# A diffusion layer on one core: the first convolution piece behind the query steps, the key weights loaded with the query projection

## The chip, the core and the metric

The kernel runs on one core of a Trainium2 chip. A core has a matrix engine (TensorE, PE in the rows; its weight loads are PEld), three engines for elementwise work (VectorE is DVE, ScalarE is ACT, GpSimd is POOL), SyncE (SP), whose queue here issues nearly all loads from memory, and 16 DMA engines that carry them. Each engine runs its own list of instructions strictly in the order in which it was written. The metric is the device time of one execution in microseconds (us): 1972.51 us before, the median of three runs (1969.02 to 1973.7).

## What is computed

One layer for 512 latent tokens of width 1024, with 256 context tokens as extra keys. Cut to what the change touches:

```
h  = modulate(rms_norm(x, norm1_g), sh1, sc1);  u = h @ w_in
q  = rms_norm(u[q part]) @ w_uq                # 16 heads of 64 + 32; the 32 are rotated (rope)
ckv = rms_norm(u[kv part]) of latent and context tokens;  kn, v = ckv @ w_ukv
attn = softmax(q k^T) v                        # per head, 768 keys
y  = a * sigmoid(g)                            # a, g: two projections of h, 1024 channels each
y  = depthwise convolution of y over the tokens, width 31, then layer norm, silu, @ w_pw
x  = x + g1 * ((gate_a * (attn @ w_o) + gate_c * y) @ w_out)
# then: norm, expert retrieval (PEER) and a final norm
```

## The kernel before

Tokens stand in four tiles of 128, in two groups of two tiles. Channels stand on the partitions in eight chunks of 128 (k). Group 0 goes through attention and the merge of its branches first, then its expert part is routed and its gathers run beside group 1; the last third of the time is a dense pass over all experts for group 1. Products that need high precision are split: a float32 tile is cast to a short form on ScalarE (line 107), the rest is taken on VectorE (line 108), and three matmuls (lines 128 to 130) stand for one.

Around the change the code goes through these steps.

- `query_in` (`qsteps[0]`): the query projection of group 0, its norm, and four transposes (line 287) into `cqT`.
- The key path: `kvn` is normed and transposed (lines 449 and 453), giving `ckvT`, and the rotated key parts in the four `KT` tiles.
- `query_half` (`qsteps[1:]`, two of them): for each half of the heads, two loads of `wuq` (line 296), eight matmuls of 384 columns (line 301; each shows as two records in the trace), copies of `qn` on ScalarE (302), six rotation instructions for each of two token tiles on VectorE (310 to 315), eight transposes for each tile (line 321), and copies to `QT` (324 on VectorE, 325 on ScalarE).
- `conv_in`: eight pieces, one for each channel chunk m. A piece loads and splits `w_cg` and `w_ca`, runs 96 matmuls of 256 columns (lines 128 to 130), a sigmoid (220), the product `glu` (221 on VectorE), the first tap on ScalarE (223), 29 taps on VectorE (line 225, `yo<-glu,cvw,yo`), and the last tap in two halves (227).
- `attention`: loads `wkn` and `wv`, then 32 units of one head and one token tile. For each pair of heads `keys` makes keys and values (478, 486); a unit has scores (497), a maximum on VectorE (499), an exponential on ScalarE (501), transposes (507) and the product with the values (522). A table of fillers says behind which unit other work is given: sixteen steps of the modulation matrix (`wm`, line 173; matmuls on line 176) at every second unit, convolution pieces at units 1, 5, 9 and so on, four gate chunks (565) at units 3, 9, 15 and 21.

The order in which the code gives its steps is not yet the order on the engines: a scheduler takes all instructions and writes each engine's list, earlier given steps first where they are ready. Buffers come from pools that are handed out in a ring, in the order of the code: in this part raw weights (`wt`, `wuq`, `wm`) share three buffers, so a load has to wait until the raw weight three before it has been used or split. SP's queue holds such a load, and everything behind it, until then. `big` takes from a ring of 14 buffers of 128x1024.

Of the kernel before, what the change touches and what calls it, by code (L numbers as in the profile page):

```python
# [45 lines left out]
PIECES, POFF = 1, 1  # L46
QPOS = (0, 0, 0)
GATES, GOFF, GSTEP = 4, 3, 6
LATE, N0, NU = 6, 0, 48

GROUPS = [[0, 1], [2, 3]]
# [20 lines left out]
def tile_layer(ctx, tc, a, out):  # L72
    nc = tc.nc
    te, ve, se, ge, sy = nc.tensor, nc.vector, nc.scalar, nc.gpsimd, nc.sync
# [18 lines left out]
    def big(name, dt=F32):  # L93
        return k4.tile([P, D], dt, name=name, tag="k4")
# [25 lines left out]
    def at(x, *i):  # L120
        return tuple(t[(slice(None),) + i] for t in x)
# [84 lines left out]
    def conv_in(y):  # L206
        def piece(m):
            glu = cvb_.tile([P, SEQ + 2 * HALF], F32, name="glu")
            ve.memset(glu[:, 0:HALF], 0.0)
            ve.memset(glu[:, SEQ + HALF:], 0.0)  # L210
            wg = wload(a["w_cg"], m)
            wa = wload(a["w_ca"], m)
            pg = ps1()
            pa = ps1()
            for o, w in ((pg, wg), (pa, wa)):
                for g, x in enumerate((hh, h2nd)):
                    for k in range(KC):
                        mm3(o[:, g * GT:(g + 1) * GT], at(w, k), at(x, k), k == 0, k == KC - 1)
            sg = sp.tile([P, SEQ], F32, name="sg", tag="c2", bufs=2)
            se.activation(sg, pg, AF.Sigmoid)  # L220
            ve.tensor_mul(glu[:, HALF:HALF + SEQ], pa, sg)
            yo = cvb_.tile([P, SEQ], F32, name="yo")
            se.activation(yo, glu[:, 0:SEQ], AF.Identity, bias=cvb[:, m:m + 1], scale=cvw[:, m, 0:1])  # L223
            for w in range(1, W - 1):
                ve.scalar_tensor_tensor(yo, glu[:, w:w + SEQ], cvw[:, m, w:w + 1], yo, op0=ALU.mult, op1=ALU.add)  # L225
            for o, c in ((y[:, m], slice(0, GT)), (yo[:, GT:], slice(GT, SEQ))):
                ve.scalar_tensor_tensor(o, glu[:, W - 1 + c.start:W - 1 + c.stop], cvw[:, m, W - 1:W], yo[:, c],
                                       op0=ALU.mult, op1=ALU.add)
            sy.dma_start(yd[:, m], yo[:, GT:])
        return [lambda m=m: piece(m) for m in range(KC)]  # L230

    def conv_norm(y):

        raw = [big("sT").rearrange("p (k t) -> p k t", k=4) for _ in range(2)]
        pm = ps2()
        for k in range(KC):
            te.matmul(pm[:, :GT], ones, y[:, k], start=k == 0, stop=k == KC - 1)
        mu = sp.tile([P, GT], F32, name="mu", tag="mu", bufs=2)
        se.mul(mu, pm[:, :GT], 1.0 / D)
        for q in range(2):  # L240
            yv = y[:, 4 * q:4 * q + 4]
            ve.tensor_sub(yv, yv, mu[:, None, :].to_broadcast([P, 4, GT]))
            se.activation(raw[q], yv, AF.Square)
        pv = ps2()
        for k in range(KC):
            te.matmul(pv[:, :GT], ones, raw[k // 4][:, k % 4], start=k == 0, stop=k == KC - 1)
        rd = sp.tile([P, GT], F32, name="rd", tag="mu", bufs=2)
        se.activation(rd, pv[:, :GT], AF.Sqrt, bias=eps_t, scale=1.0 / D)
        ve.reciprocal(rd, rd)
        hi, lo = [], []  # L250
        for q in range(2):
            yv = y[:, 4 * q:4 * q + 4]
            ve.tensor_mul(yv, yv, rd[:, None, :].to_broadcast([P, 4, GT]))
            for j in range(4):
                k = 4 * q + j
                se.activation(yv[:, j] if turn["split"] else raw[q][:, j], yv[:, j], AF.Silu, bias=lnb[:, k:k + 1], scale=lng[:, k:k + 1])
            if turn["split"]:
                h, l = two(yv, lambda: big("sp", F32R).rearrange("p (k t) -> p k t", k=4))
                hi.append(h)
                lo.append(l)  # L260
        return (hi, lo) if turn["split"] else (raw,)


    def queries(tiles, hx):

        cqT = sp.tile([P, 2, GT], F32, name="cqT", tag="sgm", bufs=2)
        QT = [[None, None] for _ in tiles]
        return QT, [lambda: query_in(tiles, hx, cqT)] + [lambda hf=hf: query_half(tiles, cqT, QT, hf) for hf in range(2)]
# [23 lines left out]
    def query_half(tiles, cqT, QT, hf):  # L292
# [10 lines left out]
        for i, t in enumerate(tiles):  # L303
# [21 lines left out]
            se.copy(qv[:, :, 1], pv[:, :, 1])  # L325
            QT[i][hf] = qt


    lc = ctx.enter_context(tc.tile_pool(name="lc", bufs=1))
    cvw = lc.tile([P, KC, W], F32)  # L330
# [10 lines left out]
    pieces = conv_in(y)  # L341
# [7 lines left out]
    with tc.tile_pool(name="tmp0", bufs=1) as t0:  # L349
# [55 lines left out]
        def split_h(g, o):  # L405
            for q in range(2):
                ks = slice(4 * q, 4 * q + 4)
                se.copy(o[0][:, ks], hT[g][q])
                ve.tensor_sub(o[1][:, ks], hT[g][q], o[0][:, ks])
# [13 lines left out]
            key_in(i)  # L423
        QT, qsteps = queries(GROUPS[0], hh)
        qsteps[0]()
        split_h(1, h2nd)
        sy.dma_start(cvw, a["cvw"])
        sy.dma_start(iota, a["iota"])
# [25 lines left out]
        for i in range(2):  # L454
            ve.tensor_copy(KT[i][1][:NOPE], pk2[:NOPE, :NKV])
            se.copy(KT[i][0][NOPE:HD], pk2[NOPE:HD, :NKV])
        for f in pieces[:1]:
            f()

    ep2 = early.enter_context(tc.tile_pool(name="ep2", bufs=1, side="right"))  # L460


    def attention(tiles, QT, fillers, wide=False):
        split = turn["split"]
        wk, wv = ((big if split else wtile)(n) for n in ("wkn", "wv"))
        sy.dma_start(wk, a["wkn"])
        sy.dma_start(wv, a["wv"])
        ah = [big("ah", F32R if split else F32).rearrange("p (k t) -> p k t", k=4) for _ in range(2)]
        if split:
            al = [big("al", F32R).rearrange("p (k t) -> p k t", k=4) for _ in range(2)]  # L470
# [87 lines left out]
    def gate(c, hv, sg):  # L558

        pg = ps1()  # L560
        for j, n in enumerate(("w_ga", "w_gc")):
            w = wload(a[n], c)
            for k in range(KC):
                mm3(pg[:, j * GT:(j + 1) * GT], at(w, k), hv[k], k == 0, k == KC - 1)
        se.activation(sg, pg, AF.Sigmoid)
# [410 lines left out]
    mf = mod_fillers()  # L976
    for f in qsteps[1:]:
        f()
    for f in pieces[1:PIECES]:
        f()  # L980
    fill = {}
    for q, f in enumerate(mf):
# [5 lines left out]
    def gate_ahead(g, c):  # L988
        rd = ready[g]
        if c % 2 == 0:  # L990
            rd["t"] = ep.tile([P, D], F32, name="sg", tag="hl", bufs=2) if g else big("sg")
        rd[c] = rd["t"][:, c % 2 * 2 * GT:(c % 2 + 1) * 2 * GT]
        gate(c, [at((hb,) if g else hh, k) for k in range(KC)], rd[c])

    for c in range(GATES):
        fill.setdefault(int(GOFF + c * GSTEP), []).append(lambda c=c: gate_ahead(0, c))
    aT = attention(GROUPS[0], QT, fill)
    conv.close()
    gp = ctx.enter_context(tc.tile_pool(name="gp", bufs=GPB))
    x1 = merge(GROUPS[0], hh, aT, lambda: conv_norm(y), ready=ready[0])  # L1000
# [4 lines left out]
    QT, qsteps = queries(GROUPS[1], (hb,))  # L1005
# [6 lines left out]
    peer["it"] = gathers(res)  # L1012
    later = route(res, h2T, 1, qat)
    sT = conv_norm(y)
    aT = attention(GROUPS[1], QT, {int(GOFF + c * GSTEP): [lambda c=c: gate_ahead(1, c)] for c in range(GATES)}, True)
    x1 = merge(GROUPS[1], (hb,), aT, lambda: sT, later, ready[1])
    later[-1]()
    full, h2T, parted = back(GROUPS[1], x1, False)
# [93 lines left out]
```

## Time and profile before

| what | value |
|---|---|
| median of 3 runs | 1972.51 us |
| the profiled execution | 1971.98 us |
| its span, first to last instruction | 1970.2 us |
| PE busy | 1785.6 us (91%) |
| weight loads (PEld) busy | 1426.8 us (72%) |
| VectorE busy | 1555.2 us (79%) |
| ScalarE busy | 774.2 us (39%) |
| GpSimd busy | 760.8 us (39%) |
| mean granted clock of TensorE | 0.96 of full |

The profile is one execution. A row of the timeline gives the start and the length of a run of like instructions on one engine, with the idle time ahead of it in brackets and what ended it. The ends of matmuls are modelled: neighbouring ones overlap in the rows, so the pace of TensorE is read from start to start. The granted clock is either full (2.4 GHz, shown as 1.00) or half (1.2 GHz, shown as 0.50); values between are means over a stretch that has both. In the rows tiles have their names without numbers.

### The profile page before, as it was taken

How to read it: one execution, taken by the hardware profiler on the slowest of the kernel's cores; microseconds unless marked ns; L12 is line 12 of the kernel's file. 1: busy time of each engine (PE TensorE's matmuls, PEld its weight loads, DVE VectorE, ACT ScalarE, POOL GpSimd, SP SyncE). 2: the span in 40 equal slices, each digit the busy share in tenths (PEclk: the TensorE clock that was granted, in tenths of full speed). 3: DMA queues.
4: the chain of work that ended last, by engine and by line, in shares of the span. 5: the costliest groups of instructions: out<-in, count | busy, mean ns of one | idle time of the engine just before them, and what ended most of it. 6: DMA issues, size and time to landing. Idle time of an engine off the chain costs nothing.

```text
span 1970.2 us, 29888 instructions
## 1 busy us (share of the span) xinstructions
PE 1785.6 (91%) x10952; PEld 1426.8 (72%) x10952; DVE 1555.2 (79%) x3122; ACT 774.2 (39%) x1147; POOL 760.8 (39%) x582
## 2 busy tenths in 40 slices
PE   6889999799987999699997889999999999999997
PEld 3667777597765766573652568788888788888886
DVE  3748989755698889897687874498996478999997
ACT  5345564543225553002111344333444444444444
POOL 0000000000045776554236882276562255655660
PEclk9889999999998999799999999999999999999999
DMA  8332333368486999899877659899999899999993
GB/s 315 106 112 89 121 118 103 120 202 274 140 321 240 347 334 347 304 388 351 274 263 263 250 216 307 295 387 400 386 396 339 307 350 385 399 398 386 395 399 157
DMA packets 179011, 555.67 MB, mean 282 GB/s; under 512 B 18984, under 2 KB 49192, under 8 KB 178608
## 3 DMA queue, kind: packets, MB, share of 16 engines
q1 hardware_dynamic: 105136, 285.29, 40.2%
q0 software_dynamic: 73728, 268.47, 36.9%
q8 instruction: 86, 1.41, 0.3%
q14 instruction: 61, 0.50, 0.1%
HBM read 533.23 MB, written 20.46 MB: 281 GB/s over the span
## 4 chain that ended last, share of the span: by engine, by line
PE 49%; DVE 17%; DMA 15%; issue 10%; POOL 6%; ACT 3%; SPq 0%; DVEq 0%; POOLq 0%; ACTq 0%
PE ps L129 9%; PE ps L128 9%; PE ps L130 9%; PE ps L126 6%; DMA g<-in_u_dram,ei 5%; DMA u<-in_ut_dram 4%; DVE scu L732 3%; PE ps L497 3%; POOL ohC L848 3%; PE acc L778 3%; POOL g L729 2%; DMA g<-in_v_dram,iT 2%; DVE wp L108 2%; PE ps L522 2%; PE acc L176 2%
## 5 line engine op out<-in xcount | busy, mean ns | idle before, releaser
L729 POOL DMA_INDIRECT g<-in_u_dram,ei x256 | 343.3, 1341 | 759.8 <-DVE tk L662 537.5
L732 DVE SCALAR_TENSOR_TENSOR scu<-g,h 128x1024 bf16<-128x1024 f32 x256 | 312.5, 1221 | 40.7 <-DMA g<-in_u_dram,ei 38.0
L128 PE MATMUL ps<-h2hi,wp 128*128 128x256 f32 x1024 | 290.9, 284 | 0.0
L130 PE MATMUL ps<-h2hi,wp 128*128 128x256 f32 x1024 | 289.7, 283 | 0.4 <-DVE wp L108 0.4
L129 PE MATMUL ps<-h2lo,wp 128*128 128x256 f32 x1024 | 289.6, 283 | 0.0
L789 POOL DMA_INDIRECT g<-in_v_dram,ei x128 | 207.0, 1617 | 143.7 <-DVE vsum L795 115.7
L107 ACT CAST wp<-u 128x1024 fp32r<-128x1024 f32 x128 | 134.2, 1049 | 278.8 <-DMA u<-in_ut_dram 168.2
L773 POOL DMA_INDIRECT g<-in_v_dram,iT x128 | 133.2, 1041 | 252.9 <-PE acc L778 213.6
L108 DVE TENSOR_TENSOR wp<-u,wp 128x1024 fp32r<-128x1024 f32 x128 | 156.4, 1223 | 86.1 <-ACT wp L107 85.1
L129 PE MATMUL ps<-v,wp 128*128 128x512 f32 x512 | 205.0, 400 | 8.9 <-DVE v L108 8.9
L128 PE MATMUL ps<-v,wp 128*128 128x512 f32 x512 | 203.6, 398 | 9.5 <-ACT v L107 6.8
L128 PEld LDWEIGHTS ps<-h2hi,wp 128*128 128x128 f32 x1024 | 195.8, 191 | 12.8 <-issue 10.9
L130 PE MATMUL ps<-v,wp 128*128 128x512 f32 x512 | 203.4, 397 | 0.5
L129 PEld LDWEIGHTS ps<-h2lo,wp 128*128 128x128 f32 x1024 | 196.1, 191 | 1.8
L130 PEld LDWEIGHTS ps<-h2hi,wp 128*128 128x128 f32 x1024 | 196.0, 191 | 0.6 <-DVE wp L108 0.6
L225 DVE SCALAR_TENSOR_TENSOR yo<-glu,cvw,yo 128x512 f32<-128x512 f32 x232 | 173.2, 749 | 4.6 <-ACT yo L223 0.9
L108 DVE TENSOR_TENSOR v<-v 128x1024 fp32r<-128x1024 f32 x128 | 156.5, 1223 | 24.0 <-ACT v L107 24.0
L795 DVE SCALAR_TENSOR_TENSOR vsum<-g,act,vsum 128x1024 f32<-128x1024 f32 x127 | 163.2, 1285 | 0.8
L107 ACT CAST v<-v 128x1024 fp32r<-128x1024 f32 x128 | 132.3, 1044 | 45.2 <-PE ps L129 39.0
L778 PE MATMUL acc<-g,Wz 128*32 128x512 f32 x512 | 104.2, 623 | 23.5 <-DMA g<-in_v_dram,iT 18.6
L129 PEld LDWEIGHTS ps<-v,wp 128*128 128x128 f32 x512 | 98.1, 192 | 33.4 <-DVE v L108 14.4
L128 PEld LDWEIGHTS ps<-v,wp 128*128 128x128 f32 x512 | 98.2, 192 | 29.2 <-ACT v L107 7.4
(306 smaller groups left out, 3650.8 us busy)
## 6 DMA issues: line engine op xcount, KB each, us to landing
v<-in_v_dram SPq DMA_DIRECT2D x128, 512.0 KB, 8.5
u<-in_ut_dram SPq DMA_DIRECT2D x128, 512.0 KB, 7.8
wm<-in_wmod_dram SPq DMA_DIRECT2D x48, 512.0 KB, 4.5
wt<-in_w_pq_dram SPq DMA_DIRECT2D x32, 512.0 KB, 4.2
Gd<-gb SPq DMA_DIRECT2D x16, 928.0 KB, 4.6
gr<-Gd SPq DMA_DIRECT2D x14, 1024.0 KB, 12.2
wt<-in_w_ga_dram SPq DMA_DIRECT2D x16, 512.0 KB, 4.4
wt<-in_w_gc_dram SPq DMA_DIRECT2D x16, 512.0 KB, 3.6
```

The source lines that it names most:

```text
L107: se.copy(h, raw)
L108: ve.tensor_sub(l, raw, h)
L128: te.matmul(o, w[0], x[0], start=start, stop=False)
L129: te.matmul(o, w[0], x[1], start=False, stop=False)
L130: te.matmul(o, w[1], x[0], start=False, stop=stop)
L225: ve.scalar_tensor_tensor(yo, glu[:, w:w + SEQ], cvw[:, m, w:w + 1], yo, op0=ALU.mult, op1=ALU.add)
L729: ge.indirect_dma_start(out=g, out_offset=None, in_=a["u"], in_offset=bass.IndirectOffsetOnAxis(ap=r["ei"][:, s:s + 1], axis=0))
L732: ve.scalar_tensor_tensor(scr, g, 1.0, r["h2"], op0=ALU.mult, op1=ALU.mult, accum_out=r["act"][:, s:s + 1])
L773: ge.indirect_dma_start(out=g, out_offset=None, in_=a["v"], in_offset=bass.IndirectOffsetOnAxis(ap=r["iT"][:, tk:tk + 1], axis=0))
L778: te.matmul(acc[32 * j:32 * j + 32, 512 * c:512 * c + 512], z[:, j, 31 - i:63 - i], gs[j][:, 512 * c:512 * c + 512], start=i == 0, stop=i ...
L789: ge.indirect_dma_start(out=g, out_offset=None, in_=a["v"], in_offset=bass.IndirectOffsetOnAxis(ap=r["ei"][:, s:s + 1], axis=0))
L795: ve.scalar_tensor_tensor(r["sum"], g, w, r["sum"], op0=ALU.mult, op1=ALU.add)
```

## The change

The line of the key weights' loads is taken out of `attention` into a function of its own, which is called right behind the query projection for group 0 and in front of `attention` for group 1, as before. The first convolution piece is no longer given inside the early block but behind the two query halves. Nothing is computed otherwise.

```
+    def key_weights(alloc):
+        ws = [alloc(n) for n in ("wkn", "wv")]
+        for w, n in zip(ws, ("wkn", "wv")):
+            sy.dma_start(w, a[n])
+        return ws
...
         qsteps[0]()
+        ws = key_weights(big)
         split_h(1, h2nd)
...
-        for f in pieces[:1]:
-            f()
...
-    def attention(tiles, QT, fillers, wide=False):
+    def attention(tiles, QT, fillers, ws, wide=False):
         split = turn["split"]
-        wk, wv = ((big if split else wtile)(n) for n in ("wkn", "wv"))
-        sy.dma_start(wk, a["wkn"])
-        sy.dma_start(wv, a["wv"])
+        wk, wv = ws
...
     for f in qsteps[1:]:
         f()
-    for f in pieces[1:PIECES]:
+    for f in pieces[:PIECES]:
         f()
...
-    aT = attention(GROUPS[0], QT, fill)
+    aT = attention(GROUPS[0], QT, fill, ws)
...
+                   key_weights(wtile), True)
```

PIECES is 1, so exactly one piece stands behind the query halves and the seven others stay in the table of fillers.

SP's queue from the load of the query projection to the third convolution piece's first load, before:

```order
L117 DMA wt<-in_w_q_dram 128x1024 x2
L427 DMA cvw<-in_cvw_dram 128x248
...
L117 DMA wt<-in_w_cg_dram 128x1024
L117 DMA wt<-in_w_ca_dram 128x1024
L296 DMA wuq<-in_wuq_dram 128x768 x4
L173 DMA wm<-in_wmod_dram 128x1024 x2
...
L466 DMA wkn<-in_wkn_dram 128x1024
L467 DMA wv<-in_wv_dram 128x1024
L117 DMA wt<-in_w_ca_dram 128x1024
```

The same stretch of SP's queue now (lines behind 326 have moved by a few numbers):

```order
L117 DMA wt<-in_w_q_dram 128x1024 x2
L331 DMA wkn<-in_wkn_dram 128x1024
L331 DMA wv<-in_wv_dram 128x1024
L434 DMA cvw<-in_cvw_dram 128x248
...
L296 DMA wuq<-in_wuq_dram 128x768 x4
L117 DMA wt<-in_w_cg_dram 128x1024
L117 DMA wt<-in_w_ca_dram 128x1024
L173 DMA wm<-in_wmod_dram 128x1024 x2
```

`wkn` and `wv` moved ahead of some twenty transfers, and the first piece's two weights moved from in front of the four `wuq` to behind them.

TensorE from the end of the query projection (line 287) to the first scores, before; ps_573 and ps_574 are the first convolution piece:

```order
L287 MATMUL ps_508<-ident,cqn 128x128 x2
L128 MATMUL ps_573<-hb,wp 128x256
...
L130 MATMUL ps_574<-h2nd_120,wp 128x256
L301 MATMUL ps_716<-wuq,cqT 128x384 x2
...
L176 MATMUL acc<-wm,ccz 32x512
L321 MATMUL ps_742<-ident,qn 96x128
...
L176 MATMUL acc<-wm,ccz 32x512 x2
L478 MATMUL ps_840<-ckvT,wkn 128x384
```

The same stretch of TensorE now; ps_701 and ps_702 are the first convolution piece:

```order
L287 MATMUL ps_508<-ident,cqn 128x128 x2
L301 MATMUL ps_570<-wuq,cqT 128x384 x2
...
L321 MATMUL ps_596<-ident,qn 96x128
...
L301 MATMUL ps_644<-wuq,cqT 128x384 x2
L128 MATMUL ps_701<-hb,wp 128x256
...
L130 MATMUL ps_702<-h2nd_120,wp 128x256
L481 MATMUL ps_840<-ckvT,wkn 128x384
L176 MATMUL acc<-wm,ccz 32x512
```

The query matmuls now come first and the 96 matmuls of the piece last before the keys; twelve matmuls on `wm` that stood among the query steps now stand behind the first keys.

VectorE in the query steps and the first attention units, before:

```order
L221 TENSOR_TENSOR glu<-ps_574,sg 128x512
L225 SCALAR_TENSOR_TENSOR yo<-glu,cvw,yo 128x512 x4
L310 TENSOR_TENSOR rt<-qn,rope 128x128
L225 SCALAR_TENSOR_TENSOR yo<-glu,cvw,yo 128x512
L311 TENSOR_TENSOR rt<-qn,rope 128x128
...
L324 COPY QT<-ps_821 96x4x128
L499 TENSOR_REDUCE st<-ps_861 128x1
L499 TENSOR_REDUCE st<-ps_876 128x1
```

VectorE in the query steps and the first attention units now:

```order
L310 TENSOR_TENSOR rt<-qn,rope 128x128
L311 TENSOR_TENSOR rt<-qn,rope 128x128
...
L324 COPY QT<-ps_675 96x4x128
...
L221 TENSOR_TENSOR glu<-ps_702,sg 128x512
...
L225 SCALAR_TENSOR_TENSOR yo<-glu,cvw,yo 128x512 x5
L502 TENSOR_REDUCE st<-ps_861 128x1
...
L502 TENSOR_REDUCE st<-ps_1042 128x1
L225 SCALAR_TENSOR_TENSOR yo<-glu,cvw,yo 128x512 x20
```

The 29 taps of the first piece no longer alternate with the rotations of the queries; they stand among the maxima of the first units, and one run of 20 (of the first and the second piece together) stands behind the third maximum. From the middle of the first group's attention on (the convolution's sixth piece) the lists of all engines are the same as before, and so are all lists behind it.

## Rows read from the trace of the kernel before

**Rows 1.** The chain of waits that ended last, 75 to 125 us: shares, then start, us, what

```profile
by line: DVE yo L225 26.2%; DMA wm<-in_wmod_dram 16.7%; DMA wkn<-in_wkn_dram 14.4%; PE ps L497 6.3%; PE acc L176 6.0%; PE ps L478 5.9%; DVE wp L108 4.6%; PE ps L486 4.2%; issue 2.9%; ACT yo L223 1.6%; DVE glu L221 1.4%; DVE QT L324 1.3%; DV
...
108.97 7.20 DMA wkn<-in_wkn_dram
```

**Rows 2.** By stretch, 75-116 us: length; busy PE, PEld, DVE, ACT, POOL; clock; DMA; GB/s

```profile
75.00:82.00 7.00, 7.00 (x24) 4.19 (x23) 5.73 (x11) 2.61 (x5) 0.00 (x0) 1.00 0.29 71
82.00:91.00 9.00, 4.63 (x20) 1.47 (x18) 9.00 (x21) 1.13 (x2) 0.00 (x0) 0.99 0.64 216
91.00:98.00 7.00, 6.73 (x16) 4.02 (x16) 6.81 (x11) 3.38 (x6) 0.00 (x0) 0.52 0.43 118
98.00:105.40 7.40, 3.36 (x18) 1.14 (x18) 7.40 (x17) 2.01 (x3) 0.00 (x0) 0.94 0.66 250
105.40:116.20 10.80, 5.75 (x16) 1.88 (x16) 2.99 (x9) 0.59 (x1) 0.00 (x0) 0.50 0.66 223
```

**Rows 3.** TensorE's timeline, 32 to 119 us: start, us, line, operation, count, idle before

```profile
32.16 3.64 PE L176 MATMUL acc<-wm,ccz 128*32 128x512 f32 x32
...
60.09 1.07 PE L287 MATMUL ps<-ident,cqn 128*128 128x128 f32 x4 [2.77 <-DVE cqn L284]
...
69.47 0.28 PE L128 MATMUL ps<-hb,wp 128*128 128x256 f32 x1
...
75.02 7.90 PE L301 MATMUL ps<-wuq,cqT 128*128 128x384 f32 x24
...
84.94 1.08 PE L321 MATMUL ps<-ident,qn 128*96 128x128 f32 x8
...
90.98 1.94 PE L321 MATMUL ps<-ident,qn 128*96 128x128 f32 x8 [3.32 <-DVE qn L315]
93.19 5.07 PE L301 MATMUL ps<-wuq,cqT 128*128 128x384 f32 x8 [0.27 <-ACT qn L302]
...
116.21 2.93 PE L478 MATMUL ps<-ckvT,wkn 128*128 128x384 f32 x4 [2.35 <-DMA wkn<-in_wkn_dram]
```

**Rows 4.** VectorE's timeline, taps in a row and taps between rotations

```profile
76.86 3.12 DVE L225 SCALAR_TENSOR_TENSOR yo<-glu,cvw,yo 128x512 f32<-128x512 f32 x4 [0.88 <-ACT yo L223]
...
80.09 0.75 DVE L225 SCALAR_TENSOR_TENSOR yo<-glu,cvw,yo 128x512 f32<-128x512 f32 x1
80.76 0.28 DVE L311 TENSOR_TENSOR rt<-qn,rope 128x128 f32<-128x128 f32 x1
```

**Rows 5.** Groups of instructions, 60 to 120 us: count, busy us, mean ns, idle before

```profile
L225 DVE SCALAR_TENSOR_TENSOR yo<-glu,cvw,yo 128x512 f32<-128x512 f32 x29 | 21.7, 747 | 1.0 <-ACT yo L223 0.9
```

**Rows 6.** SyncE's timeline: the query weights' and the key weights' issues

```profile
51.66 26.46 SPq L296 DMA_DIRECT2D wuq<-in_wuq_dram  x4
...
108.97 0.48 SPq L466 DMA_DIRECT2D wkn<-in_wkn_dram  x1
```

**Rows 7.** DMA issues, 30 to 130 us: count, size, median us to landing

```profile
wt<-in_w_cg_dram SPq DMA_DIRECT2D x3, 512.0 KB, 4.6
```

**Rows 8.** ScalarE's timeline: the first cast of the query projection's weight

```profile
45.98 1.05 ACT L107 CAST wp<-wt 128x1024 fp32r<-128x1024 f32 x1
```

**Rows 9.** Busy time by stretch, attention of the first group

```profile
123.10:138.40 15.30, 15.30 (x122) 14.01 (x121) 5.16 (x7) 9.01 (x13) 0.00 (x0) 1.00 0.12 36
138.40:170.80 32.40, 32.40 (x259) 27.27 (x256) 30.40 (x48) 20.16 (x31) 0.00 (x0) 1.00 0.32 95
170.80:180.00 9.20, 7.28 (x47) 4.03 (x45) 6.51 (x8) 5.09 (x8) 0.00 (x0) 0.81 0.53 195
180.00:271.00 91.00, 91.00 (x708) 74.36 (x709) 83.58 (x131) 49.54 (x79) 0.00 (x0) 1.00 0.30 95
271.00:346.00 75.00, 75.00 (x563) 56.80 (x562) 66.80 (x100) 40.00 (x64) 0.00 (x0) 1.00 0.35 113
```

**Rows 10.** VectorE's timeline: a maximum behind the second piece's last tap

```profile
170.80 0.96 DVE L499 TENSOR_REDUCE st<-ps 128x1 f32<-128x768 f32 x1 [0.60 <-PE ps L497]
```

**Rows 11.** SyncE's waits, 30 to 200 us: in total, times, longest

```profile
SPq L173 <- DVE wp L108: 57.9, 6, 20.5
```

More of the change, by code (lines that the diff above doesn't have):

```diff
@@ L1014, in tile_layer @@
     sT = conv_norm(y)
-    aT = attention(GROUPS[1], QT, {int(GOFF + c * GSTEP): [lambda c=c: gate_ahead(1, c)] for c in range(GATES)}, True)
+    aT = attention(GROUPS[1], QT, {int(GOFF + c * GSTEP): [lambda c=c: gate_ahead(1, c)] for c in range(GATES)},
+                   key_weights(wtile), True)
     x1 = merge(GROUPS[1], (hb,), aT, lambda: sT, later, ready[1])
```

## The prediction, made before the changed kernel ran

> **What bounds the kernel now.** I read the chain of waits first, for the stretch that the change rewrites, then the busy time by stretch, then the timelines of TensorE, VectorE and SyncE there. From 75 to 125 us the chain runs for 26.2% through the taps of the first convolution piece on VectorE, for 16.7% through loads of `wm` and for 14.4% through the load of `wkn` [rows 1]. So the reader is to see that TensorE isn't the bound there. Its busy time falls to 4.63 of 9.00 us, 3.36 of 7.40 and 5.75 of 10.80, and its clock to 0.52 and 0.50 in two of the stretches, while VectorE is busy for all of 82 to 105.4 us [rows 2]. The cause is the order on VectorE: each rotation of the queries stands between two taps, and TensorE waits 3.32 us for one of them; then the first keys wait 2.35 us for `wkn`, which SyncE issued only at 108.97 us [rows 3, 6]. The keys start at 116.21 us.
>
> From 123.1 us on it is otherwise: TensorE is busy all the time at full clock up to 170.8 us, and from 180 to 346 us again [rows 9]. VectorE is little used at first (5.16 of 15.3 us) and then nearly full: 30.40 of 32.4, 83.58 of 91, 66.80 of 75. Attention is thus bound by TensorE with VectorE close behind it.
>
> **The change part by part.**
>
> *The head, up to the first keys.* The four transposes behind the query projection start at 60.09 us, and TensorE's next matmul, now the first on `wuq`, can start at about 61.5. Before the keys it then has the following work, by pace from start to start. 32 records of line 301: 24 took 7.90 us at full clock, so 0.329 each and 10.5 in all. 32 records of transposes of the queries: 8 took 1.08, so 4.3. Twelve transposes of the key path at the same pace: 1.6. The 96 matmuls of the first piece: 48 ran from 69.47 to 75.02, so 0.116 each and 11.1 [rows 3]. That is 27.5 us. I add 1.3 us, since the clock is still at half after the idle 2.77 us (four records on `wuq` at the 0.634 each of the half-clock row less 0.329), and 1.5 us for the turns between ScalarE's copies and the rotations that nothing covers now. The keys then start at 61.5 + 30.3 = 91.8 us, 24.4 us earlier. Bounds: 27.5 without any stall (89.0), and 42 us with the whole query part at half clock (below).
>
> *The weights of the piece.* Its two loads now stand behind the four of `wuq`, and each waits for the raw weight three before it. The last `wuq` load waits for the first query matmuls (that row spans 26.46 us before, up to 78 us, for the same reason [rows 6]), so at about 66 us; `w_cg` follows when the second `wuq` is used, about 69, lands 4.6 us later [rows 7], and is split by 76. The piece begins on TensorE at about 79. The cover is 3 us; if it is gone, each further microsecond is one of the head.
>
> *The key weights.* They are issued right behind the query projection's weights, some 60 us before they are needed, into buffers of the ring that no one has used. They cost the query projection nothing as long as its weights still land in time: their first cast starts at 45.98 us without a wait [rows 8], some 12 us after the issue. The wait of 2.35 us goes. What is late next for the first keys is TensorE itself.
>
> *The moved taps.* 29 taps with 21.7 us [rows 5] leave the head and come among the first units. In a row, each feeding the next, they follow each other by 0.76 us (four from 76.86 to 79.89); ahead of a rotation the next instruction starts after 0.67 [rows 4]. So they cost 19.4 to 22.3 us of VectorE there, and I take the 21.7 of the row. The Trainium skill, "VectorE: DVE Perf Modes", section "The DRAIN you can't avoid", says that every instruction's pipeline has to run empty before the next starts, however they are chained; by it the order is worth nothing and the taps cost 21.7 us anywhere. The trace doesn't quite agree: 0.67 against 0.76. That moves the sum by 2.3 us at most.
>
> *How VectorE takes them.* The piece's matmuls end at 91.8; the product `glu` (0.7), the first tap on ScalarE (0.8) and a copy of keys ahead of it there put the first moved tap at 93.9. In front of the maximum that stands at 170.80 us before [rows 10], VectorE has the work that it had from 123.1 to 170.8 (5.16 + 30.40 = 35.6 us [rows 9]) and the 21.7: 57.3, so this maximum comes at 151.2 if VectorE never waits. TensorE alone would bring it sooner: keys at 91.8, first scores and maxima 5.4 us later at full clock (6.9 before, less half of the 2.93 of the keys' row, which ran at half clock), the same 47.7 us, and twelve matmuls on `wm` that stood in the head before and now come here, 24 records at 3.64 / 32 us [rows 3] or 2.7 us; together 147.6. VectorE decides by 3.6 us there. The gain at this point is 170.8 - 151.2 = 19.6 us.
>
> *From there to the end.* Up to the sixth piece the lists are nearly the same, and then they are the same. Before, 170.8 to 180 had a stop and half clock (7.28 of 9.20 busy, clock 0.81 [rows 9]), some 4 us of which may or may not come again; I take 1 as gained. From 180 us on TensorE was full with VectorE 8% and 11% behind, so VectorE has room for what it carries, and everything behind moves up by the same amount. Sum: 19.6 + 1, or 21 us.
>
> The profiled execution took 1971.98 us (span 1970.2), 0.5 below the median of the runs shown; 1972.0 - 21 = 1951.
>
> **The rivals.**
>
> *The query part runs at half clock (1963).* Before, these matmuls came right behind the 96 of the piece, which ran at full clock; now they come right behind an idle stretch. The records of line 301 took 0.634 us each in the row at 93.19 against 0.329, and the eight transposes at 90.98 took 1.94 against 1.08 [rows 3]. For: the clock fell to 0.50 to 0.52 in two stretches in which TensorE waited [rows 2]. Against: the query matmuls now wait on short ScalarE copies only, and 24 of them kept the full clock before. Price: 32 x 0.305 less the 1.3 already counted, and 32 x 0.11: 12 us, a gain of 9.
>
> *VectorE is the bound and takes the taps one for one (1969).* The gain of the head, 24.4, less 21.7 leaves 3 us. For: VectorE is at 92% from 180 to 271. Against: from 123.1 to 138.4 it had 10 us idle [rows 9], into which taps fit. The Trainium skill, "Perfetto Trace Analysis", section "Identifying the Most-Contended Engine", points the same way: matmul busy time says little of how near TensorE is to its limit, weight loads say more, and for VectorE the occupancy counts; here the weight loads have 74.36 of 91 us and VectorE 83.58, so by that rule VectorE is the bound of attention. By starts, though, the matmuls of the trace follow each other without gaps, so I give it little.
>
> *TensorE sets everything (1945).* 24.4 + 1.5 for the first scores at full clock - 2.7 for the twelve matmuls + 4 for the stop that does not come again: 27 us. It needs VectorE's interleaving to go better than the count of work says.
>
> *The splits of the weights come late, and it is slower (1981).* A split is an instruction on VectorE in line with the taps; now a run of 20 taps, 13 to 15 us, stands ahead of some, and each late split holds its raw buffer and with it SyncE's whole queue. SyncE waited 57.9 us in six waits for such splits already before, 20.5 in the longest [rows 11], mostly hidden. If the next three pieces each stop TensorE for the mean of 9.7 us, 29 us are lost and 20 gained: 9 slower. It decides from the point at which a piece's second weight isn't split when its first 48 matmuls end. Against: the code's order gives the early splits ahead of the run of 20.
>
> *The change doesn't act (1969 to 1972).* The queries would stay late because their own `wuq` loads come late. The last of these loads waits for the first query matmuls, not for the piece, so little speaks for it; it shares a chance with the one-for-one case, which gives the same time.
>
> **How the numbers follow.** The forecast 0.60, half clock 0.16, VectorE one for one or no effect 0.09, TensorE alone 0.10, late splits 0.05. The forecast's own range is a gain of 15 to 26 us, 1946 to 1957. To hold eight in ten the range takes in the half-clock case and TensorE alone: 1943 to 1966; left out are the one-for-one case, the slow one and the tails, some 17%. Faster by over 0.3% (5.9 us, about what a measurement can tell from no change) are the forecast, TensorE alone, nearly all of the half-clock case and a part of the one-for-one case: 0.87. Within 0.3% is the rest of that case, 0.08; slower, the late splits, 0.05.
>
> **What would show it.** In the profile after, the first keys start at 90 to 93 us and wait for no load; the query matmuls stand at 61 to 79 us with a clock near 1.00 after the first 3 us; VectorE is busy without a break from about 94 to 151 us; the maximum behind the second piece's last tap stands near 151; from the sixth piece on every row stands about 21 us earlier. It is wrong if the keys start behind 100 us, if TensorE has waits of several microseconds for splits or exponentials between 100 and 180 us, or if what is gained at the keys has shrunk below 10 us by 180 us of the run before.

## The result, and the profile after

The changed kernel takes 1952.89 us, the median of four runs (1949.24 to 1957.35), beside 1973.11 for four runs of the kernel before on the same chip: ratio 0.9895, 95% interval 0.987 to 0.9921. The forecast was 1951, range 1943 to 1966. A second measurement of the same kernel gave 1955.15 beside 1976.19, ratio 0.9897 [0.9869, 0.9926]. By medians the gain is 20.2 and 21.0 us; 21 was predicted.

The profiled execution was the longest of its four, 1957.35 us (span 1955.5), and that of before lay 1.1 us under the median of the four. Single executions of one kernel differ by several microseconds, so below I compare places in the program.

TensorE's timeline after (start, length, line, operation, count, idle before), from the transposes behind the query projection to the first keys; it answers to [rows 3]:

```profile
60.16 0.70 PE L287 MATMUL ps<-ident,cqn 128*128 128x128 f32 x4 [2.04 <-DVE cqn L284]
61.30 2.16 PE L301 MATMUL ps<-wuq,cqT 128*128 128x384 f32 x4 [0.44 <-DVE cqT L289]
...
65.69 4.73 PE L301 MATMUL ps<-wuq,cqT 128*128 128x384 f32 x14
70.56 1.05 PE L321 MATMUL ps<-ident,qn 128*96 128x128 f32 x8
...
72.97 4.04 PE L301 MATMUL ps<-wuq,cqT 128*128 128x384 f32 x12
76.54 0.57 PE L128 MATMUL ps<-hb,wp 128*128 128x256 f32 x1
...
90.31 0.81 PE L481 MATMUL ps<-ckvT,wkn 128*128 128x384 f32 x2
```

The query matmuls follow right behind the transposes, the piece's first matmul comes at 76.54, and the keys start at 90.31 without a load in front of them, 25.9 us earlier than at 116.21. From 61.30 on no row of the stretch, shown or not, has an idle time in brackets.

SyncE's timeline after, which answers to [rows 6, 7]:

```profile
33.65 1.53 SPq L331 DMA_DIRECT2D wkn<-in_wkn_dram  x1
...
41.23 26.27 SPq L296 DMA_DIRECT2D wuq<-in_wuq_dram  x4
69.80 0.33 SPq L117 DMA_DIRECT2D wt<-in_w_cg_dram  x1
74.45 0.33 SPq L117 DMA_DIRECT2D wt<-in_w_ca_dram  x1
```

The key weights are now under way at 33.65 us. The piece's weight is issued at 69.80; the last `wuq` still waits for the first query matmuls.

Busy time by stretch after (length; PE, PEld, DVE, ACT, POOL; clock; DMA; GB/s). These answer to [rows 2, 9]:

```profile
60.00:75.00 15.00, 14.26 (x59) 9.50 (x60) 10.21 (x31) 6.08 (x11) 0.00 (x0) 0.89 0.23 61
75.00:82.00 7.00, 6.88 (x49) 5.80 (x48) 5.71 (x16) 3.48 (x6) 0.00 (x0) 1.00 0.75 234
82.00:92.00 10.00, 10.00 (x76) 8.64 (x75) 1.92 (x2) 3.95 (x5) 0.00 (x0) 1.00 0.30 100
92.00:104.00 12.00, 12.00 (x83) 9.53 (x82) 11.73 (x16) 9.77 (x16) 0.00 (x0) 1.00 0.38 132
104.00:124.00 20.00, 20.00 (x163) 16.09 (x161) 19.79 (x29) 8.99 (x13) 0.00 (x0) 1.00 0.34 107
124.00:138.00 14.00, 11.22 (x79) 6.60 (x72) 13.33 (x24) 8.21 (x16) 0.00 (x0) 1.00 0.51 163
138.00:152.00 14.00, 14.00 (x113) 12.84 (x113) 12.19 (x21) 5.54 (x8) 0.00 (x0) 1.00 0.14 46
...
160.00:251.00 91.00, 90.45 (x708) 74.16 (x706) 84.00 (x131) 48.90 (x76) 0.00 (x0) 1.00 0.37 124
```

From 92 to 138 us VectorE is all but full (44.85 of 46 us). TensorE is full too, but for 2.78 us between 124 and 138, which it spends in four waits for ScalarE: 1.05 and 0.56 for copies of keys, 0.79 and 0.39 for exponentials. Then TensorE leads again. VectorE's timeline after shows what stood in front in that gap, and the maximum that answers to [rows 10]:

```profile
93.20 3.90 DVE L225 SCALAR_TENSOR_TENSOR yo<-glu,cvw,yo 128x512 f32<-128x512 f32 x5
...
112.07 0.95 DVE L502 TENSOR_REDUCE st<-ps 128x1 f32<-128x768 f32 x1
112.94 13.33 DVE L225 SCALAR_TENSOR_TENSOR yo<-glu,cvw,yo 128x512 f32<-128x512 f32 x20
...
128.50 0.95 DVE L502 TENSOR_REDUCE st<-ps 128x1 f32<-128x768 f32 x1
...
138.35 0.95 DVE L502 TENSOR_REDUCE st<-ps 128x1 f32<-128x768 f32 x1
...
140.99 6.27 DVE L225 SCALAR_TENSOR_TENSOR yo<-glu,cvw,yo 128x512 f32<-128x512 f32 x8
...
150.49 0.96 DVE L502 TENSOR_REDUCE st<-ps 128x1 f32<-128x768 f32 x1 [0.53 <-PE ps L500]
```

Twenty taps stand in one row, the last taps of the first piece in turn with taps of the second, and the fourth maximum is behind them. Against the same maximum of before, the first ten come earlier by 26.1, 25.9, 27.0, 13.9, 22.9, 20.1, 20.3, 24.7, 23.2 and 23.0 us. So the row of taps takes 13 us from the fourth maximum alone: the fifth is 22.9 earlier again, the sixth and seventh 20, and those behind 23 to 25.

The end of attention is read at the first matmul of the convolution's norm (line 237). In before, then in after (count, shortest/median/longest ns, first and last start):

```profile
L237 PE MATMUL ps<-y,ones x32: 377/379/382, 369.8 to 543.4; 128*128 128x256 f32 x32
```

```profile
L237 PE MATMUL ps<-y,ones x32: 377/379/382, 347.5 to 521.0; 128*128 128x256 f32 x32
```

22.3 us earlier at the first norm and 22.4 at the second. In the second profile of the changed kernel the first is at 346.3, a gain of 23.5. Behind that, in the gathers, the place moves from execution to execution: the last transposes on `h` (line 635 before, 638 after) are 12.4 and 13.1 us earlier in the two profiles, the first matmul with `ohC` (849, 852) 19.1 and 15.8. I read the experiments at line 237, which the two profiles of one kernel reproduce to 1.2 us, and beside it the ratio. These 1.2 us lie ahead of the query steps: the transposes of line 287 start at 60.16 in one profile and at 58.84 in the other, and counted from there the two agree to 0.2. In the profiles of this document that start lies anywhere from 58.84 to 61.80, so the table gives the gain counted from it as well.

### The profile page after: what moved, and what is told of

Its sections match the earlier page's. It is cut to its first block, busy times and chain, and to the rows that moved or that the text cites. A ratio compares the mean times of both kernels' runs of the same rounds, so it can differ in the third digit from the quotient of the medians.

```text
span 1955.5 us, 29880 instructions
## 1 busy us (share of the span) xinstructions
PE 1779.7 (91%) x10952; PEld 1426.0 (73%) x10952; DVE 1555.0 (80%) x3122; ACT 773.8 (40%) x1147; POOL 760.9 (39%) x582
## 4 chain that ended last, share of the span: by engine, by line
PE 46%; DVE 17%; DMA 15%; issue 12%; POOL 7%; ACT 2%; SPq 0%; another core or an unknown queue 0%; DVEq 0%; POOLq 0%; ACTq 0%
PE ps L129 9%; PE ps L128 9%; PE ps L130 9%; DMA g<-in_u_dram,ei 5%; POOL g L732 4%; DMA u<-in_ut_dram 3%; DVE scu L735 3%; DMA g<-in_v_dram,iT 3%; PE ps L500 3%; PE acc L781 3%; DVE vsum L798 2%; POOL ohC L851 2%; DMA v<-in_v_dram 2%; PE ps L525 2%; PE ps L852 2%
## 5 line engine op out<-in xcount | busy, mean ns | idle before, releaser
L129 PEld LDWEIGHTS ps<-v,wp 128*128 128x128 f32 x512 | 97.8, 191 | 34.7 <-DVE v L108 15.6
```

The source lines that it names most:

```text
L129: te.matmul(o, w[0], x[1], start=False, stop=False)
```

## The experiments

| kernel | first keys, us | line 237, us | gain there | gain counted from line 287 | ratio to before (95%) |
|---|---|---|---|---|---|
| before | 116.2 | 369.8 | | | 1 |
| the change | 90.3 / 89.1 | 347.5 / 346.3 | 22.3 / 23.5 | 22.3 / 22.2 | 0.9895 [0.987, 0.9921] / 0.9897 [0.9869, 0.9926] |
| key weights early alone | 100.7 | 357.8 | 12.0 | 13.5 | 0.9934 [0.9912, 0.9957] |
| piece later alone | 90.2 | 351.7 | 18.1 | 17.9 | 0.9917 [0.9886, 0.9948] |
| change without the 29 taps | 87.9 | 342.3 | 27.5 | 26.7 | 0.9861 [0.9822, 0.9899] |
| change with the 29 taps twice | 89.6 | 372.3 | -2.5 | -2.9 | 1.0014 [0.9992, 1.0037] |
| before without the 29 taps | 97.7 | 352.2 | 17.6 | 19.3 | 0.9908 [0.9878, 0.9937] |
| pieces one unit later | 90.1 | 378.6 | -8.8 | -8.8 | 1.002 [0.9998, 1.0041] |
| second query half later | 83.2 | 353.6 | 16.2 | 16.9 | 0.9919 [0.9887, 0.995] |

**The key weights early, alone.** The piece stays where it was before.

```
+        for f in pieces[:1]:
+            f()
...
-    for f in pieces[:PIECES]:
+    for f in pieces[1:PIECES]:
```

> Half of the change alone: the key weights are loaded with the query projection, the first convolution piece stays in front of the query halves. Theory (the taps between the rotations make the head long, the key load only ends last there): the keys lose their wait of 2.35 us and then stand behind the matmuls on wm, so 1 to 4 us faster than before, 1969 to 1972 us, first keys at 113 to 115 us. Rival (the key load, 14.4% of the chain there, carries a large part of the gain): 7 us or more faster, 1966 us or less, first keys at or before 109 us.

The theory missed and the rival came true: 1965.56 us, the median of its runs, first keys at 100.7. TensorE's timeline of this kernel:

```profile
92.75 1.62 PE L321 MATMUL ps<-ident,qn 128*96 128x128 f32 x8 [2.76 <-DVE qn L315]
96.06 4.76 PE L301 MATMUL ps<-wuq,cqT 128*128 128x384 f32 x8 [1.68 <-ACT qn L302]
100.66 1.65 PE L483 MATMUL ps<-ckvT,wkn 128*128 128x384 f32 x4
102.23 1.04 PE L176 MATMUL acc<-wm,ccz 128*32 128x512 f32 x2
...
105.33 1.03 PE L321 MATMUL ps<-ident,qn 128*96 128x128 f32 x8
...
111.43 1.05 PE L321 MATMUL ps<-ident,qn 128*96 128x128 f32 x8
```

The wait for a rotation between taps is still there (2.76), and one of 1.68 for ScalarE's copy. But the keys, whose weights are now on the chip, stand ahead of the second half's transposes and not behind them, so TensorE has them to do while VectorE works through the taps. The first keys no longer mark the end of the head, then: the first scores come 8.0 us earlier than before (112.32 for 120.35), not 15.6. Something else moved with the keys. Before, 24 records on `wm` stood among the query steps, ahead of the keys; here it is eight, and TensorE's waits for loads of `wm` from 60 to 125 us shrank. Before, then here (total, times, longest):

```profile
PE acc L176 <- DMA wm<-in_wmod_dram: 6.7, 4, 2.9
```

```profile
PE acc L176 <- DMA wm<-in_wmod_dram: 1.3, 1, 1.3
```

The early load is worth 12.0 us at line 237 by itself, not the 2.35 us of its wait. How much of that is the keys' new place and how much that of the `wm` steps was not tried separately.

**The piece later, alone.** The loads of `wkn` and `wv` go back into `attention`.

```
-        ws = key_weights(big)
...
-        wk, wv = ws
+        wk, wv = ((big if split else wtile)(n) for n in ("wkn", "wv"))
+        sy.dma_start(wk, a["wkn"])
+        sy.dma_start(wv, a["wv"])
```

> The other half alone: the first piece is given behind the query halves, the key weights are loaded inside attention as before. Theory: with the piece out of the way SyncE reaches the key loads at about 78 us, they land by 86, and the first keys at about 90 us wait for nothing; so the time of the whole change, 1953 us within 3. Rival (the key load carries a part): 5 us or more slower than the whole change, 1958 us or more, with the first keys waiting for wkn.

The keys come at 90.25 us without a wait: the load is issued at 77.39 now, not at 108.97 [rows 6]. So the wait of 2.35 us goes with the piece alone, as the theory had it. Yet line 237 is 4.2 to 5.4 us behind the change (4.3 to 4.4 counted from line 287), which is nearer to the rival's 5 us, though not by the wait for `wkn` that the rival named. The intervals of the two ratios overlap, so this rests on one profile beside two. TensorE's waits from 90 to 160 us, then three rows of VectorE:

```profile
PE ps L505 <- ACT pr L499: 1.9, 1, 1.9
...
PE acc L176 <- DMA wm<-in_wmod_dram: 1.0, 1, 1.0
...
```

```profile
112.42 15.98 DVE L225 SCALAR_TENSOR_TENSOR yo<-glu,cvw,yo 128x512 f32<-128x512 f32 x24
...
143.07 0.29 DVE L525 TENSOR_TENSOR af<-rt,ps 128x128 f32<-128x128 f32 x1 [4.53 <-ACT rt L524]
...
144.94 0.95 DVE L497 TENSOR_REDUCE st<-ps 128x1 f32<-128x768 f32 x1
```

The row of taps ahead of the fourth maximum is longer than in the change, 24 taps in 15.98 us for 20 in 13.33, and that maximum comes at 130.64 for 128.50. TensorE waits for its exponential and then for a `wm` load, VectorE idles 4.53 us, and the sixth maximum is at 144.94 instead of 138.35. Why that row is longer and that load later was not tried by itself. The two parts alone give 12.0 and 18.1, together 22.3 to 23.5: they cover the same stop in two ways, and 7 to 9 us count twice in the sum.

**The change without the 29 taps of the first piece.**

```
-            for w in range(1, W - 1):
+            for w in range(1, W - 1) if m else ():
```

> The change, with the 29 middle taps of the first piece left out (the convolution of that chunk lacks them). Theory (VectorE decides from 94 to 151 us, by 3.6 us, and TensorE then): 3 to 7 us faster than the change, 1946 to 1950 us. Rival 1 (VectorE takes the taps one for one): 21.7 us faster than the change, 1931 us. Rival 2 (TensorE sets everything): no difference, 1953 us.

This is within the theory's 3 to 7 us: 5.2 us earlier at line 237 than the change's first profile, 4.0 than its second; 2.4 and 1.2 of that are there at the keys already. (The intervals of the ratios overlap here too.) The busy times of this kernel, and of the change for the like stretch:

```profile
88.00:147.00 59.00, 59.00 (x437) 46.52 (x438) 40.22 (x61) 34.95 (x51) 0.00 (x0) 1.00 0.33 105
```

```profile
93.20:150.50 57.30, 54.52 (x410) 43.68 (x405) 54.39 (x86) 30.22 (x46) 0.00 (x0) 1.00 0.36 116
```

Without the taps TensorE is busy for every microsecond and VectorE has 19 us free; with them TensorE lacks 2.78. So 21.7 us of VectorE work cost about 3 us behind the keys: they fill what was idle. The seventh maximum, which stood at 170.80, shows nearly the same, 3.9: it comes 56.3 us behind the first keys here (144.23) and 60.2 in the change.

**The same taps twice.**

```
-            for w in range(1, W - 1):
+            for w in (list(range(1, W - 1)) * (1 if m else 2)):
```

> The change, with the 29 middle taps of the first piece made twice (the convolution of that chunk has them double), 21.7 us more on VectorE. Theory (VectorE has 3 us idle left from 93 to 151 us and about 17 up to 354, which the order can reach only in part): 8 to 20 us slower than the change, 1961 to 1973 us. Rival 1 (one for one from the first tap on): 21.7 us slower, 1975 us. Rival 2 (TensorE sets everything): no difference, 1953 us.

24.8 to 26 us later than the change: more than the theory's 8 to 20, and more than the 21.7 of the first rival. VectorE's and TensorE's timelines:

```profile
112.97 39.18 DVE L225 SCALAR_TENSOR_TENSOR yo<-glu,cvw,yo 128x512 f32<-128x512 f32 x59
...
155.04 0.95 DVE L502 TENSOR_REDUCE st<-ps 128x1 f32<-128x768 f32 x1
```

```profile
115.56 1.56 PE L500 MATMUL ps<-KT,QT 128*128 128x512 f32 x4
...
136.43 1.92 PE L176 MATMUL acc<-wm,ccz 128*32 128x512 f32 x4 [3.60 <-DMA wm<-in_wmod_dram]
142.24 1.92 PE L176 MATMUL acc<-wm,ccz 128*32 128x512 f32 x4 [3.89 <-DMA wm<-in_wmod_dram]
...
157.07 1.54 PE L510 MATMUL ps<-ident,pr 128*128 128x128 f32 x6 [7.23 <-ACT pr L504]
```

The row of 20 taps has become one of 59, 25.9 us longer. Nineteen of the first piece's taps stand ahead of it in both kernels. Only 29 were added, so at least ten of the 39 by which it grew are taps of the second piece that now stand ahead of this maximum too. The scores for the fourth maximum start at 115.56, as in the change (115.81), but their maximum comes at 155.04, 26.5 us late. TensorE has other work up to 132 us, spends the next stretch on `wm` as its loads come in one by one, then waits 7.23 us for the exponential. The next maxima stay 26 to 29 us behind. Behind the row VectorE is not full; its busy time is the third of the five:

```profile
155.00:180.00 25.00, 22.35 (x158) 18.55 (x158) 15.96 (x28) 12.53 (x18) 0.00 (x0) 0.83 0.30 90
```

So the whole delay is there at the end of the row, while VectorE has 9 us free right behind it: the cost is one for one because the work stands in one row ahead of a maximum on which TensorE waits, and not because VectorE lacks room later.

**The kernel before without those taps.** The edit of the loop is the same, on the kernel before.

> The kernel before, with the 29 middle taps of the first piece left out (the convolution of that chunk lacks them); its 96 matmuls and its loads stay in front of the query halves and the key weights are loaded late. Theory (the taps between the rotations, on VectorE, make the head long): the rotations follow each other at once, first keys at 98 to 104 us instead of 116, 10 to 16 us faster than before, ratio 0.992 to 0.995. Rival 1 (the late load of the key weights makes it long, as the run with that part alone, 13 us faster, suggests): first keys still at 112 us or later, 4 us faster at most. Rival 2 (the matmuls and loads of the piece in front of the query part make it long): the same 4 us at most, with TensorE waiting for wuq.

The keys come about where the theory had them, at 97.67 for 98 to 104, and the gain is just above the top of its range, 16.2 us by medians. TensorE's timeline:

```profile
97.67 2.93 PE L478 MATMUL ps<-ckvT,wkn 128*128 128x384 f32 x4 [3.97 <-DMA wkn<-in_wkn_dram]
```

The 18.5 us that the keys gain are those of the taps between the rotations, with all that hung on them: the lists differ here too, with eight records on `wm` ahead of the keys for 24, and TensorE waits for no load of `wm` up to 125 us. What is left of the old head is the wait for `wkn`, now 3.97 us. In the old place these taps cost 17.6 us at line 237 (19.3 counted from line 287), in the new one 4 to 5.

**The changed kernel again.**

> The changed kernel once more, beside the three others of this call, as what they are compared with: 0.989 of the time before, first keys at 90 us.

Its numbers are in the table; they give the spread.

**Two tries at a better one.** The pieces one unit later:

```
-PIECES, POFF = 1, 1
+PIECES, POFF = 1, 2
```

> The change, with the seven other pieces one unit later (POFF 2 instead of 1), so that VectorE has a unit more for the first piece's taps before the second piece's come. Theory (VectorE is at its limit from 93 to 151 us and costs TensorE one wait of 3.3 us and some more there): 2 to 5 us faster than the change, ratio to it 0.9975 to 0.999. Rival 1 (the sum of VectorE's work up to the end of attention decides, not its place): no difference. Rival 2 (the last piece's taps now end behind the last unit and hold up the convolution's norm): 3 to 8 us slower than the change.

A miss, and beyond the second rival too: no better than before. Line 237 overstates it here, since 52 more of TensorE's records stand ahead of that line than in the change; at the last matmul on values of the first group (375.9 us, 349.9 and 350.3 in the change, 372.2 before) it is 26 us later than the change, and by medians 25. A row of VectorE's waits from 90 to 380 us, and two rows of its timeline:

```profile
DVE glu L221 <- PE ps L130: 23.4, 6, 9.1
```

```profile
268.03 0.49 DVE L227 SCALAR_TENSOR_TENSOR y<-glu,cvw,yo 128x256 f32<-128x256 f32 x1
...
277.74 0.69 DVE L221 TENSOR_TENSOR glu<-ps,sg 128x512 f32<-128x512 f32 x1 [3.54 <-PE ps L130]
```

In the change VectorE waits 6.4 us in four waits for such products; its row of the waits, and two rows of its timeline:

```profile
DVE glu L221 <- PE ps L130: 6.4, 4, 3.1
```

```profile
178.25 0.69 DVE L221 TENSOR_TENSOR glu<-ps,sg 128x512 f32<-128x512 f32 x1
...
184.94 0.48 DVE L227 SCALAR_TENSOR_TENSOR y<-glu,cvw,yo 128x256 f32<-128x256 f32 x1
```

There a piece's product comes before the last tap of the piece ahead for four of seven pieces, as in these rows; with the shift for one of seven. VectorE runs dry between pieces, and the maxima come at uneven distances. Why the scheduler parts them is not shown; the pieces then stand at the even units, where the `wm` steps are.

The second query half as a filler behind unit 4:

```
-    for f in qsteps[1:]:
-        f()
+    qsteps[1]()
...
+    fill.setdefault(4, []).append(qsteps[2])
```

> The change, with the second half of the queries (heads 8 to 15, not needed before unit 16) given as a filler behind unit 4. Theory (TensorE and VectorE are both full from the first keys on, so work that moves behind them costs there what it saves in front): first keys 8 to 10 us earlier, at 80 to 82 us, and the time the same as that of the change within 3 us. Rival (the head's length decides): 8 us faster than the change, ratio to it 0.996.

The keys start at 83.2 us, 6 to 7 earlier than in the change and not 8 to 10, and line 237 comes 6 to 7 us later. The rival, 8 us faster, did not show; the medians (1958.81 for 1955.15) put it 4 us behind the change, with intervals that overlap. TensorE's timeline:

```profile
131.76 1.56 PE L301 MATMUL ps<-wuq,cqT 128*128 128x384 f32 x4 [0.73 <-DVE af L530]
133.52 2.85 PE L301 MATMUL ps<-wuq,cqT 128*128 128x384 f32 x8 [0.20 <-ACT qn L302]
```

The half stands between the fifth maximum (124.51) and the sixth (146.99; 138.35 in the change). Seven of its twelve rotation instructions (135.87 to 144.25 us on VectorE) stand between taps again, as before the change. So a short head alone decides nothing. None of the versions that compute the same beats the change.

## Why the prediction was right

*What bounded the head.* Right: without the taps the old head is 18.5 us shorter at the keys. One thing was passed over: in sum TensorE's largest waits in the old head were those for loads of `wm`, 6.7 us in four, beside 3.9 for rotations and 2.35 for `wkn`. With the taps out, or with the piece moved, none of them is left ahead of the keys.

*The head's sum.* 27.5 + 1.3 + 1.5 from 61.5 gave 91.8; measured 29.0 from 61.30, or 90.31, and 89.1 in the second profile. The half clock at the start was there (0.89 in 60 to 75 us), and the rest of the query part ran at full clock (1.00), so the rival of a whole query part at half clock fell. The turns cost nearly nothing on TensorE: the piece's matmuls began at 76.54, not 79, ahead of the last two groups of transposes and around them. Small slips in the terms all but cancelled: four records at 0.305 us more are 1.2, not 1.3; the twelve transposes of the key path were slow at the start as well (0.21 us from start to start); and the 0.135 for a transpose, a row's length over its count, is 0.11 from start to start, which is 1 us over 44 of them. In the rival's favour the prediction named two stretches at half clock "in which TensorE waited"; in one of them, 91 to 98 us, TensorE was busy for 6.73 of 7.00 us [rows 2], and the wait of 3.32 lay ahead of it.

*The piece's weights.* The issue was forecast at 69 and came at 69.80; the first split ended on VectorE at 75.7, forecast at 76. The cover held, but with 0.9 us to the piece's first matmul and not 3, since the piece began earlier.

*The key weights.* This is the step whose size was off. Their wait was priced at 2.35 us and their early load otherwise at nothing. The wait would have gone with the piece alone, and the load has a worth that I had not seen: 12.0 us alone, where it lets the keys stand earlier in TensorE's list, and 4 to 5 on top of the moved piece, where the keys start at the same time with or without it and the difference comes behind them. The forecast came out right all the same, since the head was summed from TensorE's work with all stops gone. That the early loads cost the query projection nothing held: its first cast starts at 45.5 to 47.1 us in the profiles with them and at 46.0 to 47.3 in those without.

*The moved taps and VectorE.* First tap 93.9, measured 93.20; the maximum at 151.2, measured 150.49, a gain of 20.3 for 19.6. "VectorE decides by 3.6 us" was measured as 3.9: the maximum comes 60.2 us behind the keys, 56.3 without the taps; 2.78 of it are waits of TensorE, all from 124 to 138. VectorE was to be busy without a break; it was for 54.39 of 57.3 us, and at 150.49 it waited 0.53 us for TensorE. That 57.3 us passed all the same is luck: the work was 2.9 us less than counted and the breaks 2.9 us more than none. The range of 19.4 to 22.3 us for the taps was also read loosely: the 0.76 us is a mean over three taps that feed the next (0.79) and a last one ahead of a rotation (0.67), and 29 times 0.76 are 22.0. So the one-for-one rival fell for this amount of taps: their cost is 4 to 5 us in all. The rule of the Trainium skill that pointed to it ("Perfetto Trace Analysis", "Identifying the Most-Contended Engine") did not decide here, although VectorE had the higher occupancy in this stretch than TensorE's weight loads (54.39 against 43.68 us): by the rows of starts both engines were near their limit, and the run with the taps twice shows that the order decided.

*From there on.* Of the 4 us of the stop after 170.8, 1 was counted; it did not recur, and the next maximum gained 4.4 more. With that and small losses later 22.3 to 23.5 stood at line 237, where 21 was expected. The medians show 20 to 21, so 1 to 3 us of it are not seen at the end; behind line 237 the places move by as much between the two profiles, and where they went stays open.

*The other rivals.* Late splits: SyncE's issues of `wm` waited 22.9 us in eight waits for them, the longest 9.4, instead of 57.9 [rows 11], and from 90 to 354 us TensorE waited for no split. The change did act: the query matmuls start at 61.30 and wait for no load. TensorE alone (1945) is the case of the taps left out: 342.3 at line 237, ratio 0.9861.

## What to carry to other kernels

Elementwise work that stands between the steps of a chain on the same engine costs nearly its full length: here 17.6 to 19.3 of 21.7 us. Moved behind the point where the matrix engine has work of its own, the same work cost 4 to 5. Look at the longest unbroken row of it ahead of a result that the matrix engine waits for: doubled, the moved work lengthened that row and cost at least one for one. A load that is on the chip early can be worth more than its wait, since the scheduler may then place its user, and what stood in front of it, elsewhere. Of two parts that cover the same stop the gains do not add. And count from the last place that the versions share: profiles of one kernel can differ by more than a microsecond before the changed stretch begins.

## What the runs showed of the hardware

Taps of two pieces that alternate follow each other faster than taps of one piece, each of which reads the one before: 20 in 13.33 us and 59 in 39.18 are 0.66 us from start to start ((13.33 - 0.75) / 19), eight of one piece in 6.27 are 0.79 ((6.27 - 0.75) / 7). One tap lasts 0.75. The Trainium skill, "VectorE: DVE Perf Modes", section "The DRAIN you can't avoid", lets the next instruction start only when the pipeline is empty, finds nothing won by chaining without semaphores, and adds that an instruction that is not held starts earlier. In these rows a tap that reads the one before starts after it has ended and an independent one about 0.08 us ahead of that end; what holds the first was not tried. So the order is not without worth, as the prediction took the section to say: a chain costs a fifth more here. The two pieces together thus took less of VectorE than two rows one after the other would.
